# The first expert's rows picked by TensorE, and a weight ring of 17 slots, in a decoder trunk with sparse experts

## The chip, the cores and the metric

One core of a Trainium2 chip. Times are device microseconds (us) of one execution of the whole program. Before: 545.99 us, the median of three runs (545.39, 545.99, 547.07).

## The reference, cut to what matters

One sequence of 512 tokens with 1024 features, one layer, float32. A conditioning vector gives shift, scale and gate rows. A token mixer (convolution, gated recurrence, gated linear attention) is added to the residual first; it is not touched here. Then comes a mixture of experts: a group router picks one of 4 groups per token, an expert router picks two of the 4 experts in it, and the token's row goes through those two.

```python
h = rms_norm(x, g_ffn) * (1 + sc2) + sh2
# comb: 512 x 4 x 4, two entries per token that are not zero
for g in range(4):
    a   = einsum("bsd,edf->bsef", h, w_gate[g])       # 4 experts, 1024 -> 512
    up  = einsum("bsd,edf->bsef", h, w_up[g])
    hid = silu(a) * up * comb[:, :, g, :, None]
    y  += einsum("bsef,efd->bsd", hid, w_down[g])     # 512 -> 1024
x = x + gt2 * y
out = rms_norm(x, g_final)
```

Each of the 16 experts has three matrices of 2 MB, 96 MB in all, and each is read once.

## The kernel before, in words

**Experts and units.** The kernel computes only the rows that the router sends to an expert. Experts 0 to 2 are done first, in fixed order; the other 13 are ranked on the chip by how many tokens they have. The 8 units 0 to 7 (`alone`) have one expert each, with room for 128 rows, and compute in a split of each float32 into two parts (`mm3`, L81: three matmuls; `split`, L86: ScalarE casts the high part, VectorE subtracts). Units 8 to 11 have two experts each with room for 64 rows, and plain float32 matmuls. A branch (L1285) holds a slow path for counts that do not fit; it is not taken with these inputs, but all engines read its condition and pass it.

**The weight ring.** A chunk is half a matrix, 1 MB: 128 partitions of 8 KB. There are 96 chunks, in the order of use: gate and up of a unit, then down of the unit before. `load_chunk(i)` (L955) takes the next buffer of `rings[i % nring]` and issues one DMA on SP's queue; it also waits until load `i - 3` has landed. `nring` is 16: thirteen slots in pools made while the mixer ends (L922 to L924), and three in `ring2`, made on the left side (L1065) where the mixer's last tiles lay. Chunks 0 to 8 are issued while the mixer ends (L973), 9 to 11 behind the output projection (L1048), 12 and 13 behind the slots of unit 2 (L1254). Chunk 14 waits for the count limit `cntmax` (`counted`, L1256), chunk 15 for a small activation behind the branch (`warmed`, L1480, L1496). Later chunks are issued as their slot is freed: by the second quarter's split (L1274) or by the matmuls of `spent` (L1383).

**From the projection to the first expert.** `route(i)` and `rows(i)` (L1025, L1036) make the logits of a tile of 128 tokens and its normalised rows `xa`, which are stored to `h2_dram`; the four `xa` are tiles of the pool `late`. VectorE picks group and experts; TensorE's position matmuls (`ppos`, L1127) give each token its slot number at its expert (`posm`). For experts 0 and 1, `onehot` (L117) compares slot numbers with a ramp, `slot_rows` (L124) turns that into token numbers `sidx` with 8 small matmuls, and `gather` (L1133) fetches the rows from `h2_dram` with an indirect DMA on GpSimd's queue. Behind that are written the counting matmuls (`pcnt`, L1149), the count limit, the combination weights, `keep_busy` (L141: float matmuls of ones whose result is not used), the weights and slots of units 0 to 2, the first split of chunk 0, and `rank_experts` (L1167). Then comes the branch, and behind it the loop over the units. `xtrans(u)` (L1363) transposes the gathered rows of a unit, 8 transposes of 128 columns taken in steps of eight, and splits them; `proj` multiplies them with gate and up.

**What sets the order.** Nothing here is ordered by hand but for `issue_after` and the listed waits. A planner plays the program through and gives each engine, when it is free, the earliest written instruction whose inputs and buffers are ready. PSUM has six banks of the tag `pz` (`big`) and two of the tag `ps` (`small`), given in written order. The branch is planned as a whole: what is written behind it stays behind.

Of the kernel before, what the change touches and what calls it, by code (L numbers as in the profile page):

```python
# [17 lines left out]
P = 128  # L18
# [28 lines left out]
def trunk_kernel(  # L47
# [27 lines left out]
    def big(name):  # L75
        return pbank("pz", 6, name)
# [846 lines left out]
    add_ring(4, "ring1b")  # L923
    rings[:] = rings[4:] + [rings[n] for n in (2, 0, 1, 3)]  # L924


# [19 lines left out]
    raws = {}  # L946
    nring = len(rings) + 3

# [23 lines left out]

    for i in range(nring - 7):  # L973
        load_chunk(i)
# [12 lines left out]
    ss2 = late.tile([P, NT], F32, name="ss2")  # L987
    xas = [late.tile([P, D], F32, name=f"xa{i}") for i in range(NT)]
    pls = {}
# [54 lines left out]
    for i in range(2):  # L1044
        yres(i, 1, py[i])
    py = project((2, 3), [lambda i=i: [route_half(n, 0) for n in (i, i + 1)] for i in (0, 2)]
                 + [lambda i=i: route(i) for i in (0, 1)])
    for i in range(nring - 7, EARLY):  # L1048
        load_chunk(i)
# [5 lines left out]
    for i in range(2, NT):  # L1055
        rows(i)


# [5 lines left out]
    lts.close()  # L1064
    add_ring(3, "ring2", side="left")  # L1065
    mw = ctx.enter_context(tc.tile_pool(name="mw", bufs=3, reuse_waits="tile"))
# [66 lines left out]
    def gather(e):  # L1133
# [114 lines left out]

    keep_busy(5)
    for u in range(2):  # L1250
# [25 lines left out]

    keep_busy(2)
    with tc.issue_after(last_w.ins):
# [6 lines left out]
    with tc.If(many > 0):  # L1285
        bcast(gt2, mod_dram[3])
        with tc.tile_pool(name="ov", bufs=1) as ov:
# [6 lines left out]
            with tc.For_i(0, NE, 1) as e:  # L1294
                pe_ = ov.tile([P, NT], F32, name="ov_pos")
                te = ov.tile([P, NT, 1, 3], BF16, name="ov_tab")
                we = ov.tile([P, NT, 1], F32, name="ov_we")
                nc.vector.tensor_copy(pe_, pos[:, :, bass.ds(e, 1)].rearrange("p i e -> p (i e)"))
                nc.vector.tensor_copy(we, cw[:, :, bass.ds(e, 1)])
                in_three(te, we, we)  # L1300

                def weights(w, k, name):
                    t = ov.tile([P, k, 4096 // k], F32, tag="ov_w", name=name)
                    nc.sync.dma_start(t, w[bass.ds(e, 1)].rearrange("e (k p) n -> p (e k) n", p=P))
                    return t
                with tc.For_i(0, NT, 1):
                    si = ov.tile([P, 1], U32, tag="ov_si", name=f"ov_si")
                    sw = ov.tile([P, 1], F32, tag="ov_sw", name=f"ov_sw")
# [3 lines left out]
                    g = ov.tile([P, D], F32, tag="ov_g", name=f"ov_g")  # L1312
# [4 lines left out]
                    gx = ov.tile([P, KD, P], F32, tag="ov_x", name=f"ov_x")  # L1317
# [6 lines left out]
                    pa, pu = big(f"ov_pa"), big(f"ov_pu")  # L1324
                    for ps, w in ((pa, w_gate), (pu, w_up)):
                        w = weights(w, KD, f"ov_w")
                        for k in range(KD):
                            nc.tensor.matmul(ps, gx[:, k, :], w[:, k, :], start=(k == 0), stop=(k == KD - 1))
                    sa = ov.tile([P, DE], F32, tag="ov_sa", name=f"ov_sa")
                    nc.scalar.activation(sa, pa, AF.Silu)  # L1330
                    hid = ov.tile([P, KE, P], F32, tag="ov_hid", name=f"ov_hid")
                    nc.vector.scalar_tensor_tensor(hid.rearrange("s k p -> s (k p)"), pu, sw, sa, ALU.mult, ALU.mult)
                    pt = small(f"ov_ph")
                    for k in range(KE):
                        nc.tensor.transpose(pt[:, k * P:(k + 1) * P], hid[:, k, :], ident)
                    ht = ov.tile([P, KE, P], F32, tag="ov_ht", name=f"ov_ht")
                    nc.vector.tensor_copy(ht, pt.rearrange("p (k t) -> p k t", k=KE))
                    y = ov.tile([P, D], F32, tag="ov_g", name=f"ov_y")
                    wd_ = weights(w_down, KE, f"ov_wd")
                    for hf in range(2):  # L1340
                        ps = big(f"ov_pd{hf}")
                        for k in range(KE):
                            nc.tensor.matmul(ps, ht[:, k, :], wd_[:, k, hf * 512:(hf + 1) * 512],
                                             start=(k == 0), stop=(k == KE - 1))
                        cols = slice(hf * 512, hf * 512 + 512)
                        nc.vector.tensor_tensor(y[:, cols], ps, gt2[:, cols], ALU.mult)
                    scatter(y, si)
                    nc.vector.tensor_scalar(pe_, pe_, float(P), None, ALU.subtract)


    with ExitStack() as ms:
# [54 lines left out]
        def hid_t(u, hid):  # L1406
            pt = small(f"pht{u}")
            hv = hid.rearrange("s k p -> s (k p)").rearrange("s (p k) -> s p k", k=KE)
            for k in range(KE):
# [247 lines left out]
```

## Time and profile before

| | |
|---|---|
| median of 3 runs | 545.99 us |
| the profiled execution | 543.88 us |
| its span, first to last instruction | 542.1 us |
| PE, VectorE (DVE), ScalarE (ACT), GpSimd (POOL) busy | 504.1, 361.4, 247.7, 87.6 us |
| mean granted TensorE clock | 0.971 |
| DMA | 164.58 MB, mean 304 GB/s |

PE is TensorE's matmul row, PEld its weight loads, SP the engine whose queue issues most DMAs. A line such as L1127 is the line of the kernel; a helper's line stands for all its callers, so tiles are named as well. A matmul on plain float32 is two records, a transpose or a matmul on split parts is one. Records of matmuls are pipelined, so the length of one is more than its share of the time; a run of n records is what is read here. [...] "DMA share" is the mean busy share of 16 DMA engines.

### The profile page before, as it was taken

How to read it: one execution, taken by the hardware profiler on the slowest of the kernel's cores; microseconds unless marked ns; L12 is line 12 of the kernel's file. 1: busy time of each engine (PE TensorE's matmuls, PEld its weight loads, DVE VectorE, ACT ScalarE, POOL GpSimd, SP SyncE). 2: the span in 40 equal slices, each digit the busy share in tenths (PEclk: the TensorE clock that was granted, in tenths of full speed). 3: DMA queues.
4: the chain of work that ended last, by engine and by line, in shares of the span. 5: the costliest groups of instructions: out<-in, count | busy, mean ns of one | idle time of the engine just before them, and what ended most of it. 6: DMA issues, size and time to landing. Idle time of an engine off the chain costs nothing.

```text
span 542.1 us, 7915 instructions
## 1 busy us (share of the span) xinstructions
PE 504.1 (93%) x2811; PEld 341.1 (63%) x2811; DVE 361.4 (67%) x655; ACT 247.7 (46%) x396; POOL 87.6 (16%) x125
## 2 busy tenths in 40 slices
PE   7999999999989999994689999999999999998991
PEld 6766766676657887763468778787876453333341
DVE  4644499999988757448599999999897121020237
ACT  5432587596126433333467767676775020000013
POOL 3311424000035100103110220120121010111002
PEclk9999999999999899996599999999999999999997
DMA  8995978758718299378789899999999999999973
GB/s 284 300 345 152 280 262 268 245 157 315 266 61 315 105 394 421 120 262 280 265 309 328 312 365 374 347 358 378 369 375 373 363 384 384 399 362 394 399 319 155
DMA packets 54304, 164.58 MB, mean 304 GB/s; under 512 B 12181, under 2 KB 30881, under 8 KB 39926
## 3 DMA queue, kind: packets, MB, share of 16 engines
q1 hardware_dynamic: 50710, 156.36, 78.8%
q0 software_dynamic: 3552, 7.69, 5.5%
q8 instruction: 23, 0.38, 0.3%
q14 instruction: 19, 0.16, 0.1%
HBM read 156.35 MB, written 12.62 MB: 312 GB/s over the span
## 4 chain that ended last, share of the span: by engine, by line
PE 55%; DMA 15%; DVE 12%; issue 11%; POOL 3%; ACT 2%; POOLq 0%; SPq 0%; DVEq 0%; ACTq 0%
DMA raw_u<-in_w_up_dram 6%; DMA raw_d<-in_w_down_dram 3%; DMA raw_g<-in_w_gate_dram 3%; PE py L84 2%; PE pga L84 2%; PE py L83 2%; PE pga L83 2%; PE pd L82 2%; PE pga L82 2%; PE py L82 2%; PE pup L83 2%; PE pd L83 2%; PE pd L84 2%; PE pup L84 2%; PE pup L82 2%
## 5 line engine op out<-in xcount | busy, mean ns | idle before, releaser
L1527 DVE SCALAR_TENSOR_TENSOR hid<-pup,swt,sact 128x512 f32<-128x512 f32 x12 | 8.9, 745 | 52.0 <-PE pup L1402 52.0
L507 DVE SCALAR_TENSOR_TENSOR cacc<-upad,vt,cacc 128x512 f32<-128x512 f32 x60 | 43.1, 755 | 0.1
L88 DVE TENSOR_TENSOR ml_u<-raw_u,mh_u 128x1024 fp32r<-128x1024 f32 x32 | 39.1, 1224 | 3.9 <-ACT mh_u L87 3.8
L87 ACT CAST mh_g<-raw_g 128x1024 fp32r<-128x1024 f32 x32 | 33.5, 1051 | 17.2 <-PE pga L84 12.6
L88 DVE TENSOR_TENSOR ml_g<-raw_g,mh_g 128x1024 fp32r<-128x1024 f32 x32 | 38.3, 1221 | 1.2 <-ACT mh_g L87 1.1
L87 ACT CAST mh_u<-raw_u 128x1024 fp32r<-128x1024 f32 x32 | 33.6, 1051 | 11.2 <-PE pga L84 9.0
L88 DVE TENSOR_TENSOR ml_d<-raw_d,mh_d 128x1024 fp32r<-128x1024 f32 x26 | 31.7, 1222 | 4.0 <-ACT mh_d L87 3.6
L1135 POOL DMA_INDIRECT gat<-h_rows,sidx x12 | 13.6, 1136 | 126.4 <-PE pgt L1371 70.8
L1448 PE MATMUL pd<-raw_d,ht 128*64 128x512 f32 x128 | 33.1, 600 | 0.6 <-DMA raw_d<-in_w_down_dram 0.5
L1402 PE MATMUL pup<-raw_u,xh 128*64 128x512 f32 x128 | 30.6, 596 | 2.4 <-DMA raw_u<-in_w_up_dram 2.3
L87 ACT CAST mh_d<-raw_d 128x1024 fp32r<-128x1024 f32 x26 | 27.3, 1050 | 8.1 <-PE pup L84 5.9
L1476 DVE TENSOR_TENSOR ye<-pd,gt 128x512 f32<-128x512 f32 x22 | 15.0, 689 | 22.3 <-PE pd L1448 20.8
L1402 PE MATMUL pga<-raw_g,xh 128*64 128x512 f32 x128 | 28.5, 594 | 0.0
L82 PE MATMUL pga<-mh_g,xh 128*128 128x512 f32 x64 | 27.6, 432 | 0.5 <-ACT xh L87 0.5
L83 PE MATMUL pup<-ml_u,xh 128*128 128x512 f32 x64 | 25.6, 400 | 1.6 <-DVE ml_u L88 1.5
L83 PE MATMUL pga<-ml_g,xh 128*128 128x512 f32 x64 | 26.3, 411 | 0.4 <-DVE ml_g L88 0.4
L1525 ACT ACTIVATE sact<-pga 128x512 f32<-128x512 f32 x12 | 7.2, 598 | 41.8 <-PE pga L1402 41.8
L84 PE MATMUL pga<-mh_g,xl 128*128 128x512 f32 x64 | 25.7, 402 | 0.4 <-DVE xl L88 0.4
L82 PE MATMUL pup<-mh_u,xh 128*128 128x512 f32 x64 | 25.8, 403 | 0.0
L84 PE MATMUL pup<-mh_u,xl 128*128 128x512 f32 x64 | 25.2, 394 | 0.0
L1079 POOL DMA_INDIRECT xo_rows<-ye,sidx x8 | 17.1, 2138 | 36.8 <-DVE ye L1476 36.8
L1402 PEld LDWEIGHTS pup<-raw_u,xh 128*64 128x64 f32 x128 | 9.2, 137 | 20.9 <-issue 15.1
(403 smaller groups left out, 1252.2 us busy)
## 6 DMA issues: line engine op xcount, KB each, us to landing
raw_g<-in_w_gate_dram SPq DMA_DIRECT2D x32, 1024.0 KB
raw_u<-in_w_up_dram SPq DMA_DIRECT2D x32, 1024.0 KB
raw_d<-in_w_down_dram SPq DMA_DIRECT2D x32, 1024.0 KB
wb<-in_w_ada_dram SPq DMA_DIRECT2D x16, 1024.0 KB
wa<-in_w_ada_dram SPq DMA_DIRECT2D x8, 512.0 KB
wa<-in_w_ada_dram SPq DMA_DIRECT2D x4, 1024.0 KB
raw_o<-in_w_out_dram SPq DMA_DIRECT2D x8, 512.0 KB
xin<-in_x_dram SPq DMA_DIRECT2D x4, 512.0 KB
```

Of the source, the lines that this page charges most:

```text
L82: nc.tensor.matmul(ps, lh, rh, start=start, stop=False)
L83: nc.tensor.matmul(ps, lh, rl, start=False, stop=False)
L84: nc.tensor.matmul(ps, ll, rh, start=False, stop=stop)
L87: one = nc.scalar.copy(hi, src)
L88: two = nc.vector.tensor_tensor(lo, src, hi.bitcast(F32), ALU.subtract)
L507: nc.vector.scalar_tensor_tensor(cacc[:, h, :], upad[:, h, t:t + T], w, cacc[:, h, :], ALU.mult, ALU.add)
L1079: nc.gpsimd.indirect_dma_start(out=xo_dram, out_offset=bass.IndirectOffsetOnAxis(ap=si, axis=0), in_=y, in_offset=None, bounds_check=T - 1 ...
L1135: nc.gpsimd.indirect_dma_start(out=g, out_offset=None, in_=h2_dram, in_offset=bass.IndirectOffsetOnAxis(ap=sidx[:, e:e + 1], axis=0), boun ...
L1402: nc.tensor.matmul(ps[rows_of(a)], xh[:, k, rows_of(a)], raws[used[0] + a][:, kk, :], start=(k == 0), stop=(k == KD - 1))
L1448: nc.tensor.matmul(ps[hf][rows_of(a)], ht[:, k, rows_of(a)], raws[used[0] + k // 2 * 2 + a][:, k % 2, cols(hf)], start=(k == 0), stop=(k = ...
L1476: nc.vector.tensor_tensor(y[:, cols], ps[hf], gt2[:, cols], ALU.mult)
L1527: nc.vector.scalar_tensor_tensor(prev.rearrange("s k p -> s (k p)"), pu, swt[:, u:u + 1], sa, ALU.mult, ALU.mult)
```

## The change

The four row tiles `xa` move out of the pool `late` into two tiles of 8 KB per partition of a new pool `ring3`. `ring2` gets two slots instead of three, and `ring3` is put behind it as slots 15 and 16 once the rows are read: the ring has 17 slots. The numbers of chunks that are issued early stay as they were (9, 12, 14); chunks 15 and 16 now both wait for `warmed`.

Unit 0's rows are no longer gathered and transposed. A float one-hot of the slots of expert 0 (`first_hot`, 128 tokens x 4 tiles x 128 slots) is the moving side of 32 float matmuls whose stationary side is the rows themselves, taken in steps of eight columns; the two PSUM banks that result hold the transposed rows, and `xtrans(0)` only splits them. The slots of expert 1 are now made, and its rows gathered, ahead of the slots of expert 0. A filler of 16 matmuls is put behind the last `rows`, and the fillers of 5 and 2 matmuls go.

To make room, the product of a unit's hidden layer is written over its activation (`sact`) in place of a tile of its own (`hid`), and the slow path loads half matrices; it sums the two halves in PSUM as before (left out below).

```diff
     add_ring(4, "ring1b")
     rings[:] = rings[4:] + [rings[n] for n in (2, 0, 1, 3)]
+    ring3 = add_ring(2, "ring3")
+    rings[-2:] = []
...
-    nring = len(rings) + 3
+    nring = len(rings) + 4
...
-    for i in range(nring - 7):
+    for i in range(nring - 8):
         load_chunk(i)
...
-    xas = [late.tile([P, D], F32, name=f"xa{i}") for i in range(NT)]
+    xpair = [ring3.tile([P, 2, D], F32, tag="raw", name=f"xa{i}") for i in range(2)]
+    xas = [xpair[i // 2][:, i % 2, :] for i in range(NT)]
...
-    for i in range(nring - 7, EARLY):
+    for i in range(nring - 8, EARLY):
         load_chunk(i)
...
     for i in range(2, NT):
         rows(i)
+    keep_busy(16)
...
-    add_ring(3, "ring2", side="left")
+    add_ring(2, "ring2", side="left")
+    rings.extend([ring3] * 2)
...
+    first_hot = r_([P, NT, P], "first_hot")
+    nc.vector.tensor_tensor(first_hot, iota1[:, None, :].broadcast_to((P, NT, P)),
+                            posm[:, :, 0][:, :, None].broadcast_to((P, NT, P)), ALU.is_equal)
     hots, placed = [], []
-    for e in range(2):
-        hots.append(onehot(hpool, posm[:, :, e], f"{e}"))
-        placed.append(slot_rows(hots[e:], sidx[:, e:e + 1], f"{e}"))
-        gather(e)
+    for e in (1, 0):
+        hots.insert(0, onehot(hpool, posm[:, :, e], f"{e}"))
+        placed.append(slot_rows(hots[0:1], sidx[:, e:e + 1], f"{e}"))
+        if e:
+            gather(e)
+    pg0 = []
+    for hf in range(2):
+        pt = big(f"pgt0{hf}")
+        for kk in range(4):
+            for i in range(NT):
+                nc.tensor.matmul(pt[:, kk * P:(kk + 1) * P],
+                                 xas[i].rearrange("t (p k) -> t p k", k=KD)[:, :, hf * 4 + kk],
+                                 first_hot[:, i, :], start=(i == 0), stop=(i == NT - 1))
+        pg0.append(pt)
...
-    keep_busy(5)
     for u in range(2):
         unit_weights(u, hots[u])
...
-    keep_busy(2)
     with tc.issue_after(last_w.ins):
         splits[0, 0] = split_quarter(0, 0)
...
-            gv = g.rearrange("t (p k) -> t p k", k=KD)
+            gv = g.rearrange("t (p k) -> t p k", k=KD) if u else None
             for hf in range(2):
-                pt = small(f"pgt{u}{hf}")
-                for kk in range(4):
+                pt = small(f"pgt{u}{hf}") if u else pg0[hf]
+                for kk in range(4 if u else 0):
                     k = hf * 4 + kk
                     nc.tensor.transpose(pt[:, kk * P:(kk + 1) * P], gv[:, :, k], ident)
...
-        xs = xtrans(0, gat[0])
+        xs = xtrans(0, None)
...
-            prev = me.tile([P, KE, P], F32, tag="hid", bufs=1, name=f"hid{u}")
-            nc.vector.scalar_tensor_tensor(prev.rearrange("s k p -> s (k p)"), pu, swt[:, u:u + 1], sa,
-                                           ALU.mult, ALU.mult)
+            nc.vector.scalar_tensor_tensor(sa, pu, swt[:, u:u + 1], sa, ALU.mult, ALU.mult)
+            prev = sa
```

## Rows read from the trace of the kernel before

**Rows 1.** Windows: span, busy us (x records) by engine, clock, DMA share, GB/s.
```profile
254.00:257.00 3.00, 2.44 (x23) 2.33 (x22) 2.93 (x21) 0.00 (x0) 1.50 (x2) 0.50 0.17 68
...
264.00:302.00 38.00, 35.01 (x169) 27.04 (x170) 35.57 (x47) 26.39 (x31) 3.59 (x3) 0.94 0.88 308
302.00:304.00 2.00, 2.00 (x9) 1.33 (x8) 1.95 (x4) 0.11 (x1) 0.24 (x1) 1.00 0.51 131
...
310.00:420.00 110.00, 109.92 (x561) 84.06 (x562) 100.17 (x118) 76.85 (x90) 19.59 (x12) 1.00 0.99 367
420.00:522.00 102.00, 98.76 (x450) 39.46 (x446) 15.64 (x30) 9.35 (x15) 9.04 (x7) 1.00 1.01 386
```

**Rows 2.** Chain that ended last: start, us, what.
```profile
255.19 8.76 DMA gat<-h_rows,sidx
...
502.34 8.33 DMA raw_d<-in_w_down_dram
```

**Rows 3.** Timeline at the first expert: start, us, engine, line, operation, [idle before <-releaser].
```profile
252.13 0.19 PE L1127 MATMUL ppos<-chob,utri 128*128 128x16 bf16 x1 [4.83 <-DVE chob L1123]
...
264.09 1.94 PE L1371 MATMUL pgt<-ident,gat 128*128 128x128 f32 x8 [4.01 <-DMA gat<-h_rows,sidx]
265.21 0.59 ACT L87 CAST xh<-pgt 128x512 fp32r<-128x512 f32 x1 [3.27 <-PE pgt L1371]
...
265.85 0.80 PE L82 MATMUL pga<-mh_g,xh 128*128 128x512 f32 x1
```

**Rows 4.** Windows of 1 us where the granted clock falls and rises.
```profile
247.00:248.00 1.00, 0.30 (x2) 0.19 (x2) 0.77 (x1) 0.98 (x2) 0.25 (x2) 0.98 0.88 291
...
268.00:269.00 1.00, 0.92 (x3) 0.39 (x2) 1.00 (x2) 0.77 (x2) 0.00 (x0) 0.78 0.79 197
```

**Rows 5.** Timeline of VectorE ahead of the branch, and ScalarE behind it.
```profile
252.91 1.29 DVE L120 TENSOR_TENSOR ohs<-iota,posm 128x512 bf16<-128x512 f32 x2
...
254.94 0.17 DVE L1150 COPY cnt<-pcnt 128x16 f32<-128x16 f32 x1
...
258.18 0.16 DVE L1169 SCALAR_TENSOR_TENSOR key<-cnt,iota 128x13 f32<-128x13 f32 x1
...
260.46 0.32 DVE L1180 TENSOR_REDUCE ranked<-named 1x13 int32<-1x169 f32 x1
...
261.74 0.20 ACT L1480 ACTIVATE warm<-ones 128x1 f32<-128x1 f32 x1 [3.09 <-DVEq L1285]
```

**Rows 6.** Timeline of PE: fillers at either clock, slot and counting matmuls.
```profile
14.99 1.50 PE L145 MATMUL pw<-ones 128*128 128x128 f32 x12
...
253.65 0.37 PE L130 MATMUL ptb<-ptab,ohs 128*128 128x1 bf16 x8 [1.09 <-DVE ohs L120]
...
254.49 0.25 PE L1149 MATMUL pcnt<-chob,onesb 128*128 128x16 bf16 x4
...
255.07 2.50 PE L145 MATMUL pw<-ones 128*128 128x128 f32 x10 [0.33 <-DVE sidx L132]
```

**Rows 7.** Timeline: eight transposes of contiguous columns, and in steps of eight.
```profile
225.56 1.04 PE L999 MATMUL ph<-ident,xa 128*128 128x128 f32 x8
...
296.99 1.04 PE L1371 MATMUL pgt<-ident,gat 128*128 128x128 f32 x8
```

**Rows 8.** Timeline of SP: issues of loads 14, 15, 25, 28 and 60.
```profile
256.30 0.33 SPq L964 DMA_DIRECT2D raw_d<-in_w_down_dram  x1
...
262.20 1.07 SPq L964 DMA_DIRECT2D raw_d<-in_w_down_dram  x1
...
302.77 0.33 SPq L964 DMA_DIRECT2D raw_u<-in_w_up_dram  x1
...
309.32 0.33 SPq L964 DMA_DIRECT2D raw_g<-in_w_gate_dram  x1
...
411.71 0.33 SPq L964 DMA_DIRECT2D raw_u<-in_w_up_dram  x1
```

**Rows 9.** SP's waits at 296 to 303: waited for, us in total, times, longest.
```profile
SPq L964 <- PE pd L1439: 3.1, 1, 3.1
```

More of the change, by code (lines that the diff above doesn't have):

```diff
@@ L1300, in trunk_kernel, with weights @@
                 in_three(te, we, we)
-                def weights(w, k, name):
-                    t = ov.tile([P, k, 4096 // k], F32, tag="ov_w", name=name)
-                    nc.sync.dma_start(t, w[bass.ds(e, 1)].rearrange("e (k p) n -> p (e k) n", p=P))
+                def weights(w, k, s, name):
+                    t = ov.tile([P, k // 2, 4096 // k], F32, tag="ov_w", name=name)
+                    nc.sync.dma_start(t, w[bass.ds(e, 1)].rearrange("e (k p) n -> p (e k) n", p=P)
+                                      [:, s * (k // 2):(s + 1) * (k // 2), :])
                     return t
                 with tc.For_i(0, NT, 1):
-                    si = ov.tile([P, 1], U32, tag="ov_si", name=f"ov_si")
-                    sw = ov.tile([P, 1], F32, tag="ov_sw", name=f"ov_sw")
+                    si = ov.tile([P, 1], U32, tag="ov_si", name="ov_si")
+                    sw = ov.tile([P, 1], F32, tag="ov_sw", name="ov_sw")
                     hot = [onehot(ov, pe_, f"ov")]
@@ L1311, in trunk_kernel @@
                     slot_weights(hot, [te[:, :, 0, :]], sw, f"ov")
-                    g = ov.tile([P, D], F32, tag="ov_g", name=f"ov_g")
+                    g = ov.tile([P, D], F32, tag="ov_g", name="ov_g")
                     nc.vector.memset(g, 0.0)
@@ L1316, in trunk_kernel @@
                                                  bounds_check=T - 1, oob_is_err=False)
-                    gx = ov.tile([P, KD, P], F32, tag="ov_x", name=f"ov_x")
+                    gx = ov.tile([P, KD, P], F32, tag="ov_x", name="ov_x")
                     for hf in range(2):
@@ L1323, in trunk_kernel @@
                         nc.vector.tensor_copy(gx[:, hf * 4:hf * 4 + 4, :], pt.rearrange("p (k t) -> p k t", k=4))
-                    pa, pu = big(f"ov_pa"), big(f"ov_pu")
+                    pa, pu = big("ov_pa"), big("ov_pu")
                     for ps, w in ((pa, w_gate), (pu, w_up)):
-                        w = weights(w, KD, f"ov_w")
-                        for k in range(KD):
-                            nc.tensor.matmul(ps, gx[:, k, :], w[:, k, :], start=(k == 0), stop=(k == KD - 1))
@@ L1329, in trunk_kernel @@
-                    sa = ov.tile([P, DE], F32, tag="ov_sa", name=f"ov_sa")
+                        for s in range(2):
+                            wt = weights(w, KD, s, "ov_w")
+                            for kk in range(KD // 2):
+                                k = s * (KD // 2) + kk
+                                nc.tensor.matmul(ps, gx[:, k, :], wt[:, kk, :], start=(k == 0), stop=(k == KD - 1))
+                    sa = ov.tile([P, DE], F32, tag="ov_sa", name="ov_sa")
                     nc.scalar.activation(sa, pa, AF.Silu)
-                    hid = ov.tile([P, KE, P], F32, tag="ov_hid", name=f"ov_hid")
+                    hid = ov.tile([P, KE, P], F32, tag="ov_hid", name="ov_hid")
@@ L1332, in trunk_kernel @@
                     nc.vector.scalar_tensor_tensor(hid.rearrange("s k p -> s (k p)"), pu, sw, sa, ALU.mult, ALU.mult)
-                    pt = small(f"ov_ph")
+                    pt = small("ov_ph")
                     for k in range(KE):
                         nc.tensor.transpose(pt[:, k * P:(k + 1) * P], hid[:, k, :], ident)
-                    ht = ov.tile([P, KE, P], F32, tag="ov_ht", name=f"ov_ht")
+                    ht = ov.tile([P, KE, P], F32, tag="ov_ht", name="ov_ht")
                     nc.vector.tensor_copy(ht, pt.rearrange("p (k t) -> p k t", k=KE))
-                    y = ov.tile([P, D], F32, tag="ov_g", name=f"ov_y")
@@ L1339, in trunk_kernel @@
-                    wd_ = weights(w_down, KE, f"ov_wd")
+                    y = ov.tile([P, D], F32, tag="ov_g", name="ov_y")
+                    ps = [big(f"ov_pd{hf}") for hf in range(2)]
+                    for s in range(2):
+                        wd_ = weights(w_down, KE, s, "ov_wd")
+                        for kk in range(KE // 2):
+                            k = s * (KE // 2) + kk
+                            for hf in range(2):
+                                nc.tensor.matmul(ps[hf], ht[:, k, :], wd_[:, kk, hf * 512:(hf + 1) * 512],
+                                                 start=(k == 0), stop=(k == KE - 1))
@@ L1340, in trunk_kernel @@
                     for hf in range(2):
[L1341 to L1344, printed above, removed]
                         cols = slice(hf * 512, hf * 512 + 512)
-                        nc.vector.tensor_tensor(y[:, cols], ps, gt2[:, cols], ALU.mult)
+                        nc.vector.tensor_tensor(y[:, cols], ps[hf], gt2[:, cols], ALU.mult)
@@ L1407, in hid_t @@
             pt = small(f"pht{u}")
-            hv = hid.rearrange("s k p -> s (k p)").rearrange("s (p k) -> s p k", k=KE)
+            hv = hid.rearrange("s (p k) -> s p k", k=KE)
             for k in range(KE):
```

## The prediction

> **What bounds the kernel now.** I read the windows first [rows 1]. From 310 us to 522 the share of the DMA engines is 0.99 to 1.01. Ahead of that it is 0.17 at 254 to 257, 0.88 at 264 to 302 and 0.51 at 302 to 304. PE is full from 310 to 420 too. Then the chain that ended last [rows 2]: late in the span it stands on loads of expert weights one behind the other, the last of them a `raw_d` from 502.34 to 510.67. So the weight stream sets the end. An edit helps if the stream has done more by the time it is full (near 310), and hurts if the DMA engines stand longer before. A shift of PE's own work counts through the ring slots that it frees. Behind the last load of the chain 31.4 us are left to the span's end (510.67 to 542.1); the change touches there only which slots the output rows take, and those loads are queued on SP behind the last weight load as before.
>
> Then the stretch around the change, instruction by instruction. PE has nothing for 4.83 us up to 252.13 [rows 3], and the clock falls meanwhile, at about 248.0 [rows 4]. The one-hots are built from 252.91 on [rows 5]; the rows of unit 0 are gathered from 255.19 to 263.95 [rows 2], transposed from 264.09, and the first expert matmul starts at 265.85 [rows 3]. But the gather is not alone there: DVE works until 260.78 at counting and ranking ahead of the branch, and ScalarE's first instruction behind the branch waits for DVE until 261.74 [rows 5]. Even with rows that cost nothing the start could come only some 3 us earlier.
>
> **The change part by part.**
>
> *The filler of 16 matmuls* is 32 records and falls into PE's idle time from 247.3 on. At full clock a record takes 1.50/12 = 0.125 us, at half 2.50/10 = 0.25 [rows 6]: 4.0 us, hidden, done by 251.3; at half 8.0, done by 255.3, and the position matmuls come 3.2 late. I take the first. The fillers removed (14 records, 10 of them 2.50 us) lay beside DVE's work: nothing.
>
> *The float one-hot* is one more DVE operation of 128x512; a pair takes 1.29 us [rows 5], so 0.65. It stands first, and PE can start on the rows at 253.7.
>
> *Picking the rows*: 2 halves x 4 column groups x 4 token tiles = 32 float matmuls of 128 columns, so 64 records. 1.50/12 has the last one's tail in it, which 64 records bear once: I take 0.115 each, 7.4 us. The two slot groups, 0.37 each [rows 6], slip in between: 0.7. At full clock the end is 253.7 + 8.1 = 261.8. If the clock is low at the start, the trace's own rise is the measure: it came some 4.4 us after PE took up unbroken work (264.09, [rows 3]; 0.78 between 268 and 269, [rows 4]). 4.4 us do 18 records at 0.25, the other 46 take 5.3, and the end is 264.1. I take 262.5, nearer the full clock, since the filler covers 4 of the 4.83 us.
>
> The stationary operand is read in steps of 32 bytes. Rows show no price for it: eight transposes with such a step took 1.04 us, eight of contiguous columns 1.04 [rows 7]. [...]
>
> *What is queued behind.* The planner gives an engine the earliest written instruction that is ready. The counting matmuls are written behind the rows, and their PSUM bank comes free only with the slot matmuls; the rows are ready before. So I expect counting behind all 64 records. From its start to the count it is 0.45 us (254.49 to 254.94, [rows 5, 6]), from there to load 14, which waits for the limit, 1.36 (256.30, [rows 8]): load 14 goes out at 262.5 + 1.8 = 264.3, 8 us late. Ranking starts from the same count: 0.17 for it, 2.6 by its rows (258.18 to 260.78), and 0.6 for the weights and slots of units 0 to 2, which come late too. DVE ends at 266.3; the branch is 0.96 later (260.78 to 261.74), at 267.3. Then 0.25 for the small activation, and 0.64 from the cast of the rows to the first matmul (265.21 to 265.85, [rows 3]): 268.2. The expert loop starts 2.3 us later than before, although the gather and 1.94 us of transposes are gone from its path. DVE is nearly full from there on and PE full to 420 [rows 1], so the 2.3 us stay with PE and with every slot that it frees.
>
> *The ring.* Slots 15 and 16 wait for the rows to be read (262.5) and for the small activation: 267.3 + 0.46 = 267.7, against 262.20 for load 15 before [rows 8]. From then on load n waits for the slot of n-17, not n-16. Before, the last wait that left the DMA engines idle is at load 25 (302.77, [rows 8]; SP waited 3.1 us for down matmuls of unit 0, [rows 9]), and load 26 stands right behind it. Afterwards that slot serves load 26, at 302.77 + 2.3 = 305.1, and load 25 has gone: one load less behind the wait. A load in the full stretch costs 3.2 us, gathers and scatters included (309.32 to 411.71 for 32, [rows 8]). So 2.3 - 3.2 = -0.9. Can the stream have done its part by then? From 264.3 it has loads 14 to 25 and half a load for the gate row: 12 x 3.2 + 1.6 = 40 us, to 304.3. Just so; a later start would bind.
>
> *At nothing:* the hidden product written over its activation (the same DVE operation; the next activation now waits for four transposes that PE does just ahead of the up matmuls, 0.5 us once per unit under a full PE if it shows); the overflow branch, not taken; unit 1's gather placed first, with some 30 us to spare; unit 0's gather gone from the DMA engines, in a stretch where they idle.
>
> **The sum**: -0.9 us. On the profiled execution, 543.88 (its span 542.1 and 1.8 around), 543.0; on the median of 545.99, which is 2.1 above it, 545.1; I say 545.0. Rows done at 261.8 give -1.6, at 264.1 +0.7.
>
> **The rivals.**
>
> A. *Counting goes ahead of the rows.* Load 14 stays at 256.5, ranking is done beside the rows, and only the weights and slots of units 0 to 2 follow (1.3 us of PE with its gaps, 0.5 to DVE's end): branch at 262.5 + 1.8 + 0.96 = 265.3, first matmul 266.2, shift +0.3, sum -2.9: 543.1. For it: counting needs no more than the position matmuls do. Against: before, it also ran only after the second slot group, though PE stood still ahead of it [rows 6].
>
> B. *The clock is half for the rows* (the slower side). 64 x 0.25 + 0.7 = 16.7: end at 270.4, 7.9 later, sum +7.0: 553. It decides from an end of 264.9 on, where the sum passes +1.5. For it: the clock fell within 0.7 us of PE's last routing matmul, and ten records at 255.07 did not bring it back [rows 4, 6]; PE has only short matmuls from 251.3 to 253.7. Against: the filler, and the rise after 4.4 us of unbroken work. A middle course, end at 266.5, gives 549.
>
> C. *The deeper ring brings nothing*: the stream starts too late to be a load ahead at 305, so the late start counts whole: 545.99 + 2.3 = 548.3. For it: there is no slack in 304.3 against 305.1. Against: the DMA engines had 0.12 x 38 = 4.6 us idle at 264 to 302 [rows 1].
>
> D. *The stride costs.* With records twice as long the rows take 14.7 us and end at 269.1: 552. The trace speaks against it [rows 7]. [...]
>
> **Chances.** Forecast 0.55 (its own range 543.6 to 547.5: -1.6 and +0.7 with the spread of the runs, 545.39 to 547.07), A 0.22, B 0.13, C 0.08, D 0.02. About 0.3%, 1.6 us, is what can be told from no change here. Faster by more: 0.3 of the forecast and 0.9 of A, 0.36. Slower by more: B, C and D but for their mildest courses, 0.19. Within: 0.45. The range for 8 in 10 runs from 541.8 (A with the rows done at full clock, and the spread) to 549.0 (B's middle course).
>
> **What would show it.** Right: counting behind the row matmuls; load 14 near 264; the last row matmul at 262 to 264, 0.23 us apiece; the first expert matmul at 267 to 269; load 26 at about 305 and no gap at 302 to 304. Wrong: counting at 255; a clock of 0.5 for all the rows; the first expert matmul ahead of 265; a DMA share under 0.95 after 310, which would mean that the stream no longer sets the end.

## The result, and the profile after

The changed kernel takes 555.14 us (median of 4 runs, 554.59 to 555.99) against 545.74 (4 runs) for the kernel before: a ratio of 1.0169, 95% interval 1.0147 to 1.0191. It is 9.4 us slower; 545.0 was forecast, with a range up to 549.0. Its profiled execution has a span of 552.9 us, 10.8 longer than before.

The windows of the changed kernel, columns as in [rows 1]:

```profile
257.00:271.00 14.00, 14.00 (x66) 13.99 (x67) 3.46 (x12) 0.00 (x0) 1.18 (x1) 1.00 0.05 14
264.00:302.00 38.00, 31.50 (x161) 25.76 (x161) 28.55 (x53) 19.80 (x24) 2.81 (x2) 0.91 0.71 273
302.00:304.00 2.00, 2.00 (x10) 1.63 (x9) 2.00 (x3) 1.82 (x3) 0.00 (x0) 1.00 0.95 291
310.00:420.00 110.00, 109.92 (x559) 85.95 (x558) 102.09 (x118) 79.36 (x93) 19.28 (x11) 1.00 0.99 366
420.00:522.00 102.00, 99.47 (x466) 41.69 (x466) 20.81 (x38) 11.99 (x18) 11.57 (x8) 1.00 1.00 377
```

From 302 us on the DMA engines are as busy as before to within 0.01, or busier. The difference lies ahead: from 257 to 271 they do next to nothing (0.05, where it was 0.79 before), while PE is full at a clock of 1.00 (TensorE's granted clock, as a share of full speed) and even its weight loads (PEld, the second pair) fill the whole window. The timeline of PE in that stretch, and the row of SP that goes with it:

```profile
247.46 6.39 PE L145 MATMUL pw<-ones 128*128 128x128 f32 x32
253.68 0.17 PE L1132 MATMUL ppos<-chob,utri 128*128 128x16 bf16 x1
...
255.12 1.69 PE L1160 MATMUL pgt<-first_hot,xa 128*128 128x128 f32 x6 [1.04 <-DVE first_hot L1147]
...
258.09 13.09 PE L1160 MATMUL pgt<-first_hot,xa 128*128 128x128 f32 x54
271.01 0.25 PE L1168 MATMUL pcnt<-chob,onesb 128*128 128x16 bf16 x4
...
276.24 0.79 PE L82 MATMUL pga<-mh_g,xh 128*128 128x512 f32 x1 [3.98 <-ACT xh L87]
```

```profile
272.84 0.33 SPq L966 DMA_DIRECT2D raw_d<-in_w_down_dram  x1
```

A row record takes 13.09/54 = 0.242 us, at full clock, and the rows end at 271.2. The counting stands behind them, load 14 goes out at 272.84 (256.30 before, [rows 8]), and the first expert matmul comes at 276.24, 10.4 us later than in [rows 3]. The filler has the clock at half for most of its length (0.50 from 247.5 to 252) and holds the position matmuls 2 us: `chob`, which they read, was ready at 251.66.

It helps to cut the span at the issue of the last weight load, here of the kernel before, of the changed one and of a run told of below (`raw_d`, start and us of the issue):

```profile
513.26 0.33 SPq L964 DMA_DIRECT2D raw_d<-in_w_down_dram  x1
```

```profile
521.66 0.33 SPq L966 DMA_DIRECT2D raw_d<-in_w_down_dram  x1
```

```profile
512.55 0.33 SPq L967 DMA_DIRECT2D raw_d<-in_w_down_dram  x1
```

Before, 542.1 - 513.26 = 28.84 us are left behind it; in the changed kernel 31.24. So of the 10.8 us 8.4 are the stream's and 2.4 were added behind the last load. The experiments follow this cut. First matmul, last load and rest are from the profiled executions, one of each kernel. Three pairs in the table are the same kernel up to the tail: r_ring_only and r_ring_tail, the changed kernel and a_tail, e1_contig and e1_tail. Their last loads differ by 1.34, 0.95 and 0.45 us, so that column is good to about 1.3 us; the rest is far steadier.

| kernel | time to before (95%) | first expert matmul | last load | rest |
|---|---|---|---|---|
| before | | 265.85 | 513.26 | 28.84 |
| changed | 1.0169 (1.0147 to 1.0191) | 276.24 | 521.66 | 31.24 |
| e1_contig | 1.0044 (1.0021 to 1.0068) | 268.33 | 512.55 | 31.15 |
| e2_count_first | 1.0173 (1.0123 to 1.0222) | 274.77 | 521.22 | 31.28 |
| e3_no_fill | 1.0192 (1.0150 to 1.0235) | 274.95 | 519.04 | 31.16 |
| r_ring_only | 1.0022 (0.9993 to 1.0051) | 266.23 | 511.12 | 31.18 |
| r_ring_tail | 0.9980 (0.9956 to 1.0003) | 266.61 | 512.46 | 28.84 |
| e1_tail | 1.0000 (0.9976 to 1.0025) | 267.90 | 513.00 | 28.90 |
| v3_rows_last | 0.9971 (0.9951 to 0.9992) | 264.25 | 510.66 | 28.84 |
| a_tail | 1.0162 (1.0125 to 1.0200) | 275.49 | 522.61 | 28.89 |
| v5_rows_ring16 | 1.0012 (0.9986 to 1.0038) | 266.51 | 515.36 | 29.04 |
| v6_best_no_fill | 0.9981 (0.9952 to 1.0011) | 265.33 | 511.40 | 29.10 |

### The profile page after: what moved, and what is told of

It is laid out like the page before. It is cut to its first block, busy times and chain, and to the rows that moved or that the text cites. A ratio compares the mean times of both kernels' runs of the same rounds, so it can differ in the third digit from the quotient of the medians.

```text
span 552.9 us, 8064 instructions
## 1 busy us (share of the span) xinstructions
PE 520.5 (94%) x2885; PEld 357.8 (65%) x2885; DVE 362.5 (66%) x656; ACT 247.0 (45%) x396; POOL 86.5 (16%) x124
## 5 line engine op out<-in xcount | busy, mean ns | idle before, releaser
L1549 DVE SCALAR_TENSOR_TENSOR sact<-pup,swt,sact 128x512 f32<-128x512 f32 x12 | 9.0, 746 | 49.9 <-PE pup L1425 49.9
L1471 PE MATMUL pd<-raw_d,ht 128*64 128x512 f32 x128 | 35.5, 600 | 1.2 <-DMA raw_d<-in_w_down_dram 1.2
L1425 PE MATMUL pup<-raw_u,xh 128*64 128x512 f32 x128 | 29.4, 596 | 1.8 <-DMA raw_u<-in_w_up_dram 1.8
L1471 PEld LDWEIGHTS pd<-raw_d,ht 128*64 128x64 f32 x128 | 10.5, 136 | 21.1 <-issue 16.5
```

The source lines that it names most:

```text
L1425: nc.tensor.matmul(ps[rows_of(a)], xh[:, k, rows_of(a)], raws[used[0] + a][:, kk, :], start=(k == 0), stop=(k == KD - 1))
L1471: nc.tensor.matmul(ps[hf][rows_of(a)], ht[:, k, rows_of(a)], raws[used[0] + k // 2 * 2 + a][:, k % 2, cols(hf)], start=(k == 0), stop=(k = ...
```

## The experiments

**Contiguous columns for the rows (e1_contig).**

```diff
-    xas[i].rearrange("t (p k) -> t p k", k=KD)[:, :, hf * 4 + kk]
+    xas[i][:, (hf * 4 + kk) * P:(hf * 4 + kk + 1) * P]
-    src.rearrange("e (p k) n -> p (e k) n", p=P)
+    src.rearrange("e (p k) n -> p (e k) n" if i >= 4 else "e (k p) n -> p (e k) n", p=P)
```

> The changed kernel, with the stationary operand of the 64 row records taken as 128 contiguous columns instead of in steps of 32 bytes; to keep the features in their places the first four weight loads (gate and up of unit 0) are read with rows 128 apart. Everything else, the filler and the counting behind the rows too, stays. Theory (the step makes a float weight load twice as long): a row record takes 0.115 to 0.125 us instead of 0.242, the last ends near 263.5 instead of 271, load 14 goes out near 265.3, the first expert matmul at about 268.7, and the time is 555.1 - 7.5 = 547.6 us. Rival 1 (TensorE really runs at half clock there, whatever the profile's clock says) and rival 2 (a float record with a new stationary operand takes 0.24 whatever its step): records stay at 0.24 and the time at 555.

Measured: 547.35 us, 1.0044. PE's timeline of this run:

```profile
255.27 0.94 PE L1161 MATMUL pgt<-first_hot,xa 128*128 128x128 f32 x6 [1.04 <-DVE first_hot L1148]
...
256.98 6.28 PE L1161 MATMUL pgt<-first_hot,xa 128*128 128x128 f32 x54
...
268.33 0.80 PE L82 MATMUL pga<-mh_g,xh 128*128 128x512 f32 x1 [4.00 <-ACT xh L87]
```

Started at the same date, the same 64 records take 7.99 us instead of 16.06, 0.116 apiece. Load 14 goes out at 264.91, the first expert matmul is at 268.33: what the forecast said from there on. The step of 32 bytes costs 8.1 us in this stretch, and both rivals (a half clock, the price of any new stationary operand) fall. On the whole time it is 1.0169 against 1.0044, that is 6.8 us, with some 2 us to either side by the two intervals.

Where the step acts is seen in PEld, TensorE's weight loads: here those of the 64 records in the changed kernel and in this run, shortest, median and longest in ns.

```profile
L1160 PEld LDWEIGHTS pgt<-first_hot,xa x64: 312/334/338, 255.1 to 270.6; 128*128 128x128 f32 x64
```

```profile
L1161 PEld LDWEIGHTS pgt<-first_hot,xa x64: 186/192/193, 255.3 to 262.9; 128*128 128x128 f32 x64
```

**Steps by themselves (e4_steps).** The edit in short:

```diff
+    keep_busy(48)
+    # 16 matmuls per group, stationary xas[j % 4][:, 0:128*step:step], moving ident
+    nc.tensor.matmul(o, st, ident, ...)          # steps 1, 2, 4, 8
+    nc.tensor.matmul(o, st, ident[:, 0:16], ...) # steps 1, 8
+    nc.tensor.transpose(o, st, ident)            # steps 1, 8
```

> The kernel before, with groups of 16 float matmuls added ahead of the positions whose results are not used: behind a filler of 48 that brings the clock up, stationary operands of 128 columns in steps of 1, 2, 4 and 8 floats with 128 moving columns, then steps of 1 and 8 with 16 moving columns, then transposes with steps of 1 and 8. The kernel gets some 30 us longer; only the time per record is looked at. Theory (a step past 16 bytes costs): 0.11 to 0.125 us per record for steps of 1, 2 and 4, 0.24 for 8; with 16 moving columns the step of 8 still takes 0.24, since the weight load binds; transposes 0.13 for both. Rival (any step costs, in proportion): 2 floats between, 4 and 8 at 0.24 or more. Rival 2 (a new stationary operand costs, not its step): 0.24 for every step.

The groups in PE's timeline, in the order above:

```profile
258.84 3.74 PE L1064 MATMUL q<-ident,xa 128*128 128x128 f32 x32
262.42 3.93 PE L1066 MATMUL q<-ident,xa 128*128 128x128 f32 x32
266.19 7.63 PE L1068 MATMUL q<-ident,xa 128*128 128x128 f32 x32
273.65 7.77 PE L1070 MATMUL q<-ident,xa 128*128 128x128 f32 x32
281.26 4.69 PE L1072 MATMUL q1n<-ident,xa 128*128 128x16 f32 x32
285.79 7.75 PE L1074 MATMUL q8n<-ident,xa 128*128 128x16 f32 x32
293.37 3.65 PE L1076 MATMUL t<-ident,xa 128*128 128x128 f32 x16
296.82 2.17 PE L1078 MATMUL t<-ident,xa 128*128 128x128 f32 x16
```

Windows of the two groups in steps of 8 floats (PE's clock is the last figure but two):

```profile
273.70:281.00 7.30, 7.30 (x32) 7.30 (x32) 0.00 (x0) 0.00 (x0) 0.00 (x0) 1.00 0.01 2
285.80:293.30 7.50, 7.50 (x33) 7.50 (x34) 0.00 (x0) 0.00 (x0) 0.00 (x0) 0.50 0.00 0
```

Per record: 0.117 and 0.123 us for steps of one and two floats, 0.238 and 0.243 for four and eight. There are two levels, and the edge lies between 8 and 16 bytes, one step earlier than expected. The strided record takes 0.24 with 128 moving columns at full clock and with 16 at half clock: neither the moving columns nor the clock set it. What the two groups share is the load of the stationary operand, which fills PEld in both windows (7.30 of 7.30 and 7.50 of 7.50 us) and lasts 334 ns in the one and 335 in the other. A contiguous operand's load in the group of 16 columns lasts 192 ns as long as the clock is at 1.00 and 333 once it is at 0.50; the fillers of the kernel before show the same (192 ns from 14.9 to 16.1 us at 1.00, 333 from 255.1 to 256.9 at 0.50). So the step takes away what the full clock gives, and at half clock it costs the load nothing; a contiguous record of 128 columns takes 0.25 us there as well ([rows 6]). The transposes' two rows stand at different clocks (0.50 and 0.90), so they say nothing of the step; the last run below does.

**Counting first (e2_count_first).** In short:

```diff
+    pc = small("pcnt")  # block moved here, ahead of first_hot, hots and the rows
...
-    pc = small("pcnt")  # from behind the rows
```

> The changed kernel, with the counting (four matmuls and its VectorE operations) written ahead of the rows; the rows keep their step of 32 bytes. Both theories expect load 14 at about 257.5 us instead of 272.84. Theory 1 (what counts is when PE starts on the experts, as PE is full from there to 420): the first expert matmul still waits for the rows and the weights and slots of units 0 to 2, about 274.6 instead of 276.24, so 555.1 - 1.6 = 553.5 us. Theory 2 (what counts is that the weight stream stood still from 257 to 273): the stream has 15 us more, and most of the loss comes back, about 547 us.

Load 14 went out at 259.54, 13 us sooner, the first expert matmul came 1.5 sooner, and the time is the same, 1.0173 against 1.0169. Theory 2, that the still stream from 257 to 273 is the loss, falls: its 547 us would be 1.002. What counts is when PE starts on the experts, and the 1.5 us it gained there are within the interval (half its width is 0.005, 2.7 us).

**Without the filler (e3_no_fill).**

```diff
-    keep_busy(16)  # behind the rows' scaling
```

> The changed kernel without the filler of 16 matmuls ahead of the positions. The positions come at about 251.7 us instead of 253.68. Theory (the row records are bound by their weight loads of 0.24 at full clock): the clock is then half when the rows start; if a strided load follows the clock they take up to 0.48 until it rises, some 18 records or 4.4 us more at first, so 555.1 - 2.0 + 4.4 = 557.5. Rival 1 (the rows already ran at half clock): records stay at 0.24, all moves 2.0 forward, 553.1 us.

554.08 us, 1.0192: no difference from the changed kernel that these intervals can tell. The theory's 557.5 us (1.0215 of the 545.74 before) lies inside the interval, the rival's 553.1 (1.0135) below it. The trace shows more: windows of the run at half and at full clock, and the row records.

```profile
256.00:258.00 2.00, 2.00 (x9) 2.00 (x10) 1.79 (x10) 0.00 (x0) 1.18 (x1) 0.50 0.00 0
260.00:262.00 2.00, 2.00 (x10) 2.00 (x10) 0.00 (x0) 0.00 (x0) 0.00 (x0) 1.00 0.00 0
```

```profile
255.83 14.04 PE L1159 MATMUL pgt<-first_hot,xa 128*128 128x128 f32 x58
```

Ten weight loads in 2 us at a clock of 0.50, ten at 1.00, 0.242 us per record throughout: the rows did not slow down at half clock, against the theory I gave, so its time inside the interval says nothing for it. The records stayed at 0.24 as the rival had it, but not for its reason, since the clock does reach 1.00.

**The ring alone (r_ring_only), and with the tail's tiles two slots on (r_ring_tail).** Against the kernel before, in short:

```diff
     rings[:] = rings[4:] + [rings[n] for n in (2, 0, 1, 3)]
+    ring3 = add_ring(2, "ring3"); rings[-2:] = []
-    nring = len(rings) + 3
+    nring = len(rings) + 4
...
-    return rings[(free[0] - 1) % nring].tile(...)  # r_ring_tail only
+    return rings[(free[0] + 1) % nring].tile(...)
```

> The kernel before with the ring of 17 alone (two slots that first hold the rows, the hidden product over its activation, the overflow branch in halves for the room); unit 0 is still gathered and transposed. Two things are weighed: what the ring gives the stream, and what it costs behind the last load. From the issue of the last weight load to the end of the span the kernel before took 28.84 us (513.26 to 542.1), the changed one 31.24 (521.66 to 552.9) and the one with contiguous columns 31.15 (512.55 to 543.7). Theory A (a load ahead is worth 3.2 us, as predicted, and the longer tail takes 2.3 back): 0.9 us under before. Theory B (the stream is full from 305 us anyway and a slot more gives it nothing; the tail costs): 2.3 us over before. Theory C (the longer tail comes from the late rows, not from the ring): tail of 28.8 and the time of before or 3.2 under it.

> The ring alone, as in the run beside it, with one difference: the tiles that the tail takes from the ring (the parts of the last two units' rows and the output rows) begin two slots further on. With that TensorE's last matmuls stand in the order of the kernel before (the matmuls that bring the rows back run in two groups between whole groups of down matmuls); without it single down matmuls stand between them. Theory (the order of the last matmuls is what makes the tail longer): the tail is 28.8 us again and the time is 2.3 us under the run beside it: before -3.2 by A, or that of before by B. Rival (the tail is longer for another reason, the slots' own dates): no difference between the two.

The ring alone is 1.0022; the last load goes out 2.1 us sooner, and 2.3 us more are left behind it. With the tail's tiles moved the rest is 28.84 again and the time 0.9980: 0.0042 or 2.3 us between the two. The longer tail is there without late rows, so C falls. How much a slot more gives the stream these two do not settle. A's 3.2 us is too much: it asks for 0.9983 and 0.9941, and both lie below the intervals. B's nothing asks for 1.0042 and 1.0000, and both lie inside; the last load was ahead by 2.1 and by 0.8 us, and that column is good to 1.3. Where the 2.3 us are is seen in PE's last matmuls (`pd` are down matmuls, `pf` those that bring the last two units' rows back to their tokens): first the kernel before, then e1_contig, which ends as all kernels with a rest of 31.2 do.

```profile
510.71 4.47 PE L1448 MATMUL pd<-raw_d,ht 128*64 128x512 f32 x16 [0.54 <-DMA raw_d<-in_w_down_dram]
515.11 2.30 PE L1575 MATMUL pf<-p,oht 128*128 128x512 f32 x7
517.34 3.65 PE L1448 MATMUL pd<-raw_d,ht 128*64 128x512 f32 x12
520.92 1.43 PE L1575 MATMUL pf<-p,oht 128*128 128x512 f32 x5
522.28 3.70 PE L1448 MATMUL pd<-raw_d,ht 128*64 128x512 f32 x16
```

```profile
509.98 4.48 PE L1472 MATMUL pd<-raw_d,ht 128*64 128x512 f32 x16 [1.46 <-DMA raw_d<-in_w_down_dram]
514.97 3.65 PE L1472 MATMUL pd<-raw_d,ht 128*64 128x512 f32 x12 [0.51 <-DMA raw_d<-in_w_down_dram]
518.55 1.43 PE L1598 MATMUL pf<-p,oht 128*128 128x512 f32 x5
519.91 1.07 PE L1472 MATMUL pd<-raw_d,ht 128*64 128x512 f32 x2
520.91 0.95 PE L1598 MATMUL pf<-p,oht 128*128 128x512 f32 x3
521.79 1.07 PE L1472 MATMUL pd<-raw_d,ht 128*64 128x512 f32 x2
522.80 1.20 PE L1598 MATMUL pf<-p,oht 128*128 128x512 f32 x4
523.92 3.65 PE L1472 MATMUL pd<-raw_d,ht 128*64 128x512 f32 x12
```

From the start of the first group to the end of the last down matmul it is 15.27 us before and 17.59 after, with the same matmuls in it. Two things make the difference. Before, seven `pf` matmuls fill the time in which the next half of the down weights lands; afterwards PE waits 0.51 us for it. And the down matmuls of a unit's two experts are records of 128*64, not of 128*128. Standing together they run side by side: in the kernel before the two that start first at 522.28 end after 0.66 us, where the changed kernel's first at 529.03 takes 0.64 alone, and the last 16 records take 3.70 us, 0.23 apiece, where a float record of 128*128 with 512 moving columns takes 0.43 (e5_steps2). Afterwards these 16 are taken apart, into 2, 2 and 12, and take 1.07 + 1.07 + 3.65 = 5.79 us: four run alone ahead, and four of the last 12 are left without a partner (in the changed kernel they start 0.43 us apart, from 534.83 to 536.12). It is an order that the planner writes, the same in all five kernels with a rest of 31.2, and moving the tail's tiles by two slots alone turns it back. Why the planner takes the other order for those slots was not looked into.

**Contiguous columns and the old order at the end (e1_tail).** The edits of e1_contig, and that of the tail.

> The changed kernel with contiguous columns for the rows (547.35 us in its run, 2.5 over before), with the tail's tiles two slots further on, so that the last matmuls stand in the order of before. Theory (the rows' late start of 2.5 us is made up by the stream, whose last load went out 0.7 us ahead of before; what is lost is the order at the end): 545.0, that is 0.7 us under before, with a tail of 28.8. Rival (the late start of PE stays to the end and makes the loss): 547.3, with 2.5 us over before.

1.0000 (0.9976 to 1.0025), rest 28.90. PE started on the experts 2.05 us late, and the last load went out 0.26 us ahead of before. So the late start does not show in the time, and the order at the end was the whole loss of e1_contig (1.0044 against 1.0000). Whether the ring made the late start up, or 2 us of start are hidden anyway, this run does not tell.

**Rows last, counting first, old order at the end (v3_rows_last).** With the edits of e1_tail and, in short:

```diff
+    pc = small("pcnt")  # counting ahead of first_hot
...
     unit_slots(2, unit_onehot(2))
+    pg0 = []  # the row matmuls, contiguous, behind the weights and slots of units 0 to 2
```

> The changed kernel with contiguous columns, the counting ahead of the rows, the rows written behind the weights and slots of units 0 to 2, and the order of before at the end. Load 14 at about 258, the last row matmul near 264.3, the first expert matmul near 266.3 (265.85 before). Theory A (start of the experts and a load ahead both count): 2 to 3 us under before, 542.5. Theory B (the stream is full from 305 and a few us at the start are hidden): the same as the run with contiguous columns and the order of before.

542.43 us, 0.9971 (0.9951 to 0.9992): faster than both kernels, by 1.6 us (0.4 to 2.7) against the one before. Its PE timeline:

```profile
252.58 0.24 PE L1149 MATMUL pcnt<-chob,onesb 128*128 128x16 bf16 x4
...
260.25 2.25 PE L1269 MATMUL pgt<-first_hot,xa 128*128 128x128 f32 x18
264.25 0.50 PE L82 MATMUL pga<-mh_g,xh 128*128 128x512 f32 x1 [1.74 <-ACT xh L87]
```

The rows end at 262.5, the branch follows at once, since counting, ranking and the weights are done beside them, and the experts start 1.6 us ahead of before instead of the 0.5 late that I expected. It is nearer to A; but the gain over e1_tail, 0.0029, is not larger than the two intervals.

**The old order at the end alone (a_tail).** The changed kernel with the tail's tiles two slots on.

> The changed kernel, rows in steps of 32 bytes and counting behind them as they are, with the tail's tiles two slots further on, so that the last matmuls stand in the order of before. Theory (the two losses add up: some 7 to 8 us from the step, 2.3 from the order at the end): 2.3 us under the changed kernel, 1.0125 of before (551.3 where before has 544.5). Rival (with PE 10 us late the order at the end no longer matters): 1.017 of before, as the changed kernel.

Inconclusive by time: 1.0162 (1.0125 to 1.0200) holds the theory's 1.0125 and the rival's 1.017. The trace has the rest at 28.89, as the theory says; but the last load went out 0.95 us later than in the changed kernel, although PE started 0.75 sooner. So of the 2.35 us 1.4 are left in the spans, and 0.4 (0.0007) in the times: with the strided rows the runs do not show what the order at the end costs.

**The rows on a ring of 16 (v5_rows_ring16).** v3_rows_last with one of the two shared slots unused and the ring counted as 16; the numbers of loads issued early stay.

```diff
-    nring = len(rings) + 4
+    nring = len(rings) + 3
-    rings.extend([ring3] * 2)
+    rings.extend([ring3])
```

> Rows picked by TensorE from contiguous columns, counting ahead of them, rows written behind the weights and slots of units 0 to 2, and a ring held at 16 half matrices (one of the two shared slots stays unused), the last matmuls in the order of before: the rows' part of the change without the deeper ring. In the run with 17 the first expert matmul came at 264.25 us (before 265.85) and the time was 0.9971 of before. Theory A (an earlier start of the experts counts whole): 1.6 us under before, 0.997. Theory B (what that run gained is the ring's): the same as before, 1.000.

1.0012 (0.9986 to 1.0038), no gain from the rows alone. A is not refuted by it, since in this profile the experts started at 266.51, 0.7 behind before. For B: the last load is 2.1 us later than before, where every kernel with 17 slots and contiguous or gathered rows has it 0.3 to 2.6 sooner. 0.9971 against 1.0012 would put the ring at 2.2 us, with intervals that just overlap. But the two runs do not differ by the ring alone: in this profile the positions came 1 us later (253.30 for 252.33), and the granted clock fell in the rows, to 0.77 from 254.8 to 257 and 0.70 from 257 to 261, where it was 1.00 in v3_rows_last from 253.8 to 262.5. So the run does not separate A from B.

**v3_rows_last without the filler (v6_best_no_fill).**

> The run with contiguous columns, counting first, rows last, ring of 17 and the order of before at the end (0.9971 of before), without the filler of 16 matmuls ahead of the positions. Theory (records of contiguous columns follow the clock, 0.25 us at half): the clock is half when the rows start, some 18 records take 0.25 until it rises, the rows end about 1.5 to 2.5 us later, and the time is 1 to 2 us over that run, 1.000. Rival (the clock is as good without it): the same time, 0.997.

0.9981 (0.9952 to 1.0011), not to be told from 0.9971. The trace shows the cost: the experts start at 265.33, 1.1 us later. Row records and clock of this run:

```profile
255.34 4.30 PE L1268 MATMUL pgt<-first_hot,xa 128*128 128x128 f32 x20
...
261.41 3.15 PE L1268 MATMUL pgt<-first_hot,xa 128*128 128x128 f32 x26
```

```profile
255.30:259.50 4.20, 4.20 (x28) 4.19 (x26) 2.90 (x13) 1.28 (x1) 1.18 (x1) 0.54 0.61 183
```

0.215 us per record at a clock of 0.54, 0.121 at 1.00 later (261.4 to 264.5): records of contiguous columns follow the clock, as the theory had it.

**Moving columns, transposes and 16-bit operands (e5_steps2).**

> The kernel before with further groups of 16 or 32 matmuls ahead of the positions, their results unused, each behind a filler that holds the clock up: float stationary operands of 128 columns in steps of 1 and 8 with 512 moving columns, transposes in steps of 1 and 8, and 16-bit stationary operands in steps of 2, 4, 8, 16 and 32 bytes with 128 moving columns. Only the time per record is looked at. Theory (the weight load binds where its columns are 16 bytes apart or more, and hides under a longer stream of moving columns): 512 columns take the same for both steps, some 0.43 us; transposes 0.13 for both; 16-bit operands the same up to 8 bytes and longer from 16 on. Rival (the price goes by the element count of the step, from 4 on): 16-bit operands get longer from 8 bytes on.

Some of the groups in PE's timeline: transposes of step 1 and 8, 16-bit operands in steps of 2 and 8 bytes and, last, of 16 and 32.

```profile
292.98 1.91 PE L1072 MATMUL t<-ident,xa 128*128 128x128 f32 x16
...
300.09 1.94 PE L1075 MATMUL t<-ident,xa 128*128 128x128 f32 x16
...
307.22 1.95 PE L1078 MATMUL b<-onesb 128*128 128x128 bf16 x32
...
321.62 1.95 PE L1084 MATMUL b<-onesb,xa 128*128 128x128 bf16 x32
...
328.82 2.10 PE L1087 MATMUL b<-onesb,xa 128*128 128x128 bf16 x32
...
336.17 2.15 PE L1090 MATMUL b<-onesb,xa 128*128 128x128 bf16 x32
```

Sixteen transposes take the same in both steps, 1.91 and 1.94 us. 16-bit operands go up from 16 bytes on, not from four elements on, and by 10% only (32 records take 1.95 us up to 8 bytes, then 2.10 and 2.15). With 512 moving columns 32 records took 13.74 us in step 1 and 13.73 in step 8 (260.15 to 273.89 and to 287.62): hidden. The theory held in all three for the time per record. The weight loads behind them do get longer everywhere, by PEld's medians: 190 to 313 ns with 512 columns, 141 to 192 for the transposes, and for 16-bit operands 98, 98, 114, 143 and 148 from 2 to 32 bytes. The transposes' 192 ns are the length of a contiguous float load, behind which records still came at 0.12 us (e1_contig).

## Why the prediction was wrong

*Picking the rows* is the step that failed: "Rows show no price for it", 0.115 us a record. It is 0.242, 8.1 us more (7.99 and 16.06 at the same start). I priced a float matmul's stationary operand by [rows 7], which are transposes, and by PE's row alone. The weight loads of the same two groups of eight show the step in the kernel before (the last figure ahead of the second bar is the mean in ns):

```profile
L999 PEld LDWEIGHTS ph<-ident,xa 128*128 128x128 f32 x8 | 0.9, 140 | 0.1
```

```profile
L1371 PEld LDWEIGHTS pgt<-ident,gat 128*128 128x128 f32 x8 | 1.0, 189 | 0.1
```

A transpose's time hides the longer load (1.04 us for eight with either load, [rows 7]), that of a float matmul with 128 moving columns does not (0.117 us a record in step 1, 0.243 in step 8, e4_steps). The rival that had it, D, got a chance of 0.02 on the strength of PE's row: its mechanism and nearly its number came true (end at 269.1 for 271.2; 552 for 555.1). That its records are twice as long no row of the kernel before shows; the runs show 0.116 us in contiguous columns (e1_contig) and 0.242 in steps of 32 bytes. A mechanism that speaks against the change deserved more than 0.02 where the only row against it is of another operation.

*Nothing at the end* failed too: "the change touches there only which slots the output rows take". It took just that, and the planner's order of the last matmuls turned with it: 2.3 us (r_ring_only and r_ring_tail, e1_contig and e1_tail). In the changed kernel itself the time does not show them (a_tail). I looked at which transfers are queued behind the last load, and not at what PE does there.

The two make the miss: with both taken out (e1_tail) the time is 1.0000 (0.9976 to 1.0025) instead of 1.0169. How the loss divides is less sure. The step is worth 6.8 us in the new order at the end (e1_contig) and 8.8 in the old one (a_tail against e1_tail), the order 2.4 us with contiguous columns and 0.4 with strided ones, each to some 2 us or a little more. That the forecast change of -0.9, and 8.1 + 2.3, are 9.5 us where the medians are 9.4 apart is luck in part: the -0.9 has a ring of 3.2 us in it, which is too much, and of the 10.4 us of later start 8.4 reached the last load.

*The range of the forecast itself*: -1.6 and +0.7 with the spread of the runs are 543.8 to 547.8, not 543.6 to 547.5; nothing hangs on it.

*The filler*: half wrong. It was neither done by 251.3 nor as late as 255.3; it ran mostly at half clock and held the positions 2 us in the changed kernel, 0.65 in the run v3_rows_last. In v5_rows_ring16 it ran at 1.00 and took 3.82 us, as forecast. With strided rows the clock it brings is worth nothing (0.242 us a record without it too, e3_no_fill), with contiguous ones 1.1 us of start, which the times do not show.

*What is queued behind*: right. Counting came behind all the rows, 1.8 us from its start to load 14, as said, and 5.1 from the rows' end to the first expert matmul (5.7 said). Rival A's order (e2_count_first) would have been worth 1.5 us of start, near the 2.0 I had for it.

*The ring*: too large, and right in kind only as far as a gain is likely. The four kernels with 17 slots, rows that do not bear the step, and the old order (r_ring_tail, e1_tail, v3_rows_last, v6_best_no_fill) are 1.1, 0.0, 1.6 and 1.0 us under before by time, 0.9 in the mean, with starts of the experts 0.2 later in the mean; 3.2 was said. Single profiles give 0.3 to 3.3 for the ten kernels with 17 slots, 1.9 in the mean, if the first expert matmul's shift is counted whole. No run separates the ring from the start of the experts for certain.

*The stream sets the end*: right as far as it goes. The last load moved by 8.4 us for 10.4 of the first expert matmul, and the DMA share stayed at 0.99 to 1.00 after 310. Only the 28.84 us behind it were not the constant that I took them for.

## What to carry to other kernels

Take the price of a strided operand from a row of the same instruction in the same role, and read the weight loads (PEld) beside the matmuls (PE); lacking such a row, let both prices stand with real chances. Where a tile ring's length or its first slot changes, compare the order of the last matmuls before and after, since the slots of the tail move too. To see such a loss, cut the span at the issue of the last weight load: the part behind it is 28.84 to 29.10 us in one order and 31.15 to 31.28 in the other, far steadier than the whole time.

## What the runs showed of the hardware

A float matmul whose 128 stationary columns lie 16 or 32 bytes apart takes 0.24 us a record with 128 moving columns, against 0.12 at 4 and 8 bytes (e4_steps, at full clock); at 32 bytes its weight load lasts 334 ns instead of 192 (changed kernel, e1_contig). The strided record takes 0.24 at clocks of 0.50 and 1.00 alike (e3_no_fill, e4_steps); at half clock the contiguous load lasts 333 ns too (e4_steps, the fillers of the kernel before). With 512 moving columns the step does not show in the time per record (13.74 and 13.73 us for 32, e5_steps2), nor does it in transposes (1.91 and 1.94 us for 16, e5_steps2), whose loads go from 141 to 192 ns; 16-bit operands show a tenth (0.061 to 0.067 us, e5_steps2). Why the load of a transpose is the shorter one stays open. In e4_steps the clock was 1.00 in the strided records up to 281.0 and in the first contiguous ones of 16 columns up to 283.0, 0.71 from 283.0 to 284.5, 0.50 from there to 296.8, and 0.90 from 296.9 to 298.8; PE had been busy without a break from 258.84 on, so it fell with no idle time before.
